# The long projection of a two-sequence encoder layer laid out beside both attentions, with other buffer counts

## The chip, the cores and the metric

The kernel runs on one core of one Trainium2 chip. Its engines are TensorE (PE, with the loads of its stationary operand shown as PEld), VectorE (DVE), ScalarE (ACT), GpSimd (POOL) and SyncE (SP), which issues the DMAs of this kernel. The metric is the device time of one execution in microseconds (us), the median of several runs.

## The reference

One layer of a bidirectional encoder is applied to two sequences with shared weights: a long one of 1024 tokens (s = 0) and a short one of 512 (s = 1), each with 16 learned meta tokens in front. The width is 1024, everything is float32.

```python
def mixer_sublayer(x, ...):
    n = rms_norm(x, g_mix)
    proj = n @ w_in                        # columns: qa, ka, va, qb, kb, vb
    # group A: 8 query heads over 2 key heads, rms-normed q and k, 2-D rotary
    s = jnp.einsum('bqhgd,bkhd->bhgqk', qblk, ka) * scale
    oa = jnp.einsum('bhgqk,bkhd->bqhgd', jax.nn.softmax(s, axis=-1), va)
    # group B: 4 differential heads, two softmax maps each, 1-D rotary
    a = p[:, :, 0] - lam * p[:, :, 1]
    ob = rms_norm(jnp.einsum('bhqk,bkhe->bqhe', a, vb), g_subln) * (1.0 - lam_init)
    return x + jnp.concatenate([oa, ob], axis=-1) @ w_out

def conv_glu_sublayer(x, ...):
    n = rms_norm(x, g_ffn)
    gate = depthwise_conv3(n @ w_ff_gate) + conv_b
    return x + (jax.nn.gelu(gate) * (n @ w_ff_up)) @ w_ff_down

# both sublayers, then rms_norm(h, g_final); the meta tokens are dropped
```

## The kernel before

Each float32 operand of the dense products is split in two halves of float32r (hi and lo), and three matmuls (`mm3`, L111 to L113) make one product: hi by hi, lo by hi, hi by lo. The work is written as Python generators, one for each stage of each sequence:

- `projection(s)` loads x, normalizes it, and makes 18 blocks of 128 columns of the combined projection: first ten for group A's q and k and for the values (each block of q or k with a per-head norm), then eight for group B's keys and queries. The long sequence has three chunks a block, 384, 384 and 272 columns wide. Results go to DRAM as `qk` and `v`.
- `attention(s)` loads keys (`k`, from pool `ak`), queries (`q`) and values (`v`) from DRAM. `softmax` makes one tile of rows `p` (pool `ap`): scores `ps_s` in PSUM (L386, L387), scaled into `p` with its maximum (L388), exponential on ACT (L393), and in group A a scaling by the inverse sum (L462). `weighted_v` transposes four such tiles (three or two in group B) key chunk by key chunk (`ps_t`, L411), splits them, and multiplies them by the values into `ps_o` (L425, L426; L421 to L423 in group B; L435 for the tail of the keys). `ps_o` has one buffer. Long attention has 16 blocks of four tiles in group A and 12 of three pairs in group B.
- `mixer_out` and `conv_glu` are the short sequence's out projection and feed-forward with its final norm. In the final norm (`finish`, L769 and on) sixteen tiles `y` are made from `h` and stored to `yT` (L785).
- `mixer_out_long` and `conv_glu_long` are the long sequence's. The first goes over three parts of the tokens. After each part `combine` makes that part's row norm and the inputs of a seven-product scheme for 2 by 2 blocks, which it keeps in tiles `x11` to `t4`. Those tiles exist from `begin()` on, which drains the short generator and releases its memory.

The order of a stage that has two generators is written with `merge`: it takes the next piece of whichever generator is less far in units that the generators yield, divided by the two weights given.

```python
    i = 0 if b is None or done[0] / wa <= done[1] / wb else 1
```

This is the order of the program text. The planner of the language then orders the instructions of each engine by an estimated timeline in which an instruction that is ready can pass an earlier one that is not; earlier text has priority. Tiles come from pools with a number of buffers, laid out from the left or the right end of on-chip memory, and an instruction that needs a buffer waits until the tile that had that memory is released. All DMAs go through one queue in order (SP).

The top level (`trunk_kernel`, L1138 and on) runs the short projection, then short attention merged with the long projection (weights `R1`) and the rest of that projection by itself, then long attention merged with the short out projection and feed-forward (`R2`), then the long out projection merged with what is left of the short stages (`R3`), then the long feed-forward. PSUM has two accumulators `mm`, three `s`, two `t` and one `o` until the long feed-forward.

Of the kernel before, what the change touches and what calls it, by code (L numbers as in the profile page):

```python
# [12 lines left out]
F32 = mybir.dt.float32  # L13
# [7 lines left out]
P = 128  # L21
# [64 lines left out]
def pool(ctx, g, name, bufs, side):  # L86
    return ctx.enter_context(g.tc.tile_pool(name=name, bufs=bufs, side=side, reuse_waits="tile"))
# [252 lines left out]
def attention(ctx, g, s, side):  # L340
# [4 lines left out]
    nch = len(kch)  # L345
    nf = n // P
    sp = pool(ctx, g, f"as{s}", 8, side)
    kp = pool(ctx, g, f"ak{s}", 4, side)
    qp = pool(ctx, g, f"aq{s}", 3, side)
    vp = pool(ctx, g, f"av{s}", 2, side)  # L350
    pp = pool(ctx, g, f"ap{s}", 9, side)
    ptp = pool(ctx, g, f"apt{s}", 3 if s == 0 else 2, side)
    op = pool(ctx, g, f"ao{s}", 2, side)
    def stacked(tl, j, m, first, c0, cw):
# [12 lines left out]
    def load_k(j, m):  # L367
        k = kp.tile([P, n], F32R, name="k", tag="k")
        stacked(k, j, m, 0, 0, n)
        return k  # L370
# [76 lines left out]
    for kv in range(2):  # L447
        k = load_k(KA, kv)
# [63 lines left out]
    for h in range(4):  # L512
# [3 lines left out]
        for blk in blocks:  # L516
# [3 lines left out]
            ob = yield from diff_block(qs, ks, v, [(c - c0, m) for c, m in blk])  # L520
# [17 lines left out]
def mean_rsqrt(g, tp, out, acc, cw, tag="mm"):  # L538
    ps = g.psum.tile(P, cw, tag)
    g.nc.tensor.matmul(ps, lhsT=g.ones_d, rhs=acc, start=True, stop=True)  # L540
    rsqrt_newton(g, tp, out, ps, cw)
# [148 lines left out]
def conv_glu(ctx, g, s, st, side, wp, wb, gb):  # L690
# [18 lines left out]
    ap = pool(ctx, g, f"fa{s}", 2, side)  # L709
    centres = even_chunks(N, 510)  # L710
    for f0 in range(0, NFF, G):
# [52 lines left out]
        op = pool(ctx, g, f"fo{s}", 2, side)  # L764
        ob = 2 - s
        cw = 256
        yv = g.yT[s].rearrange("(k p) t -> p k t", p=P)

        def finish(c0, acc, sums):  # L769
            rs = rstd[:, 1 + c0:1 + c0 + cw]  # L770
            if sums:
                rsqrt_newton(g, op, rs, acc, cw)
            else:
                mean_rsqrt(g, op, rs, acc, cw)
            for k in range(KT):
                y = op.tile([P, ob, cw], F32, name="y", tag="y", bufs=2 if s == 1 else 4) if k % ob == 0 else y
                hs, gk = h[:, k, 1 + c0:1 + c0 + cw], g.gain[:, V_GFIN + k:V_GFIN + k + 1]
                if k % 4 == 3:
                    nc.scalar.activation(y[:, k % ob], hs, AF.Copy, scale=gk)
                    nc.gpsimd.tensor_tensor(out=y[:, k % ob], in0=y[:, k % ob], in1=rs, op=ALU.mult)  # L780
                else:
                    nc.vector.scalar_tensor_tensor(out=y[:, k % ob], in0=hs, scalar=gk, in1=rs,
                                                   op0=ALU.mult, op1=ALU.mult)
                if (k + 1) % ob == 0:
                    nc.sync.dma_start(out=yv[:, k + 1 - ob:k + 1, c0:c0 + cw], in_=y)  # L785

        waiting = None
        for c0 in range(0, N, cw):
# [3 lines left out]
            for j in range(KT):  # L792
# [5 lines left out]
                else:  # L798
                    add_square(g, op, acc, h, j, 1 + c0, cw, nc.gpsimd if j < PADD else nc.vector, ob)
                if j == LAG and waiting:  # L800
                    finish(*waiting)
# [302 lines left out]
def merge(a, wa, b, wb):  # L1104

    done = [0.0, 0.0]
    while True:
        i = 0 if b is None or done[0] / wa <= done[1] / wb else 1
        try:
            done[i] += next((a, b)[i])  # L1110
        except StopIteration:
            if i == 0:
                break
            b = None


def drain(gen):
    for _ in gen:
        pass


LAG = 5
PADD = 8
ML = 2
K2 = 8
# [5 lines left out]
AF_ = 4  # L1131
LAGF = 5
TS = ("x11", "x21", "t2", "t1", "t3", "x22", "t4")
R1, R2, R3 = (1.0, 0.9), (1.0, 0.4), (1.0, 20.0)


@with_exitstack
def trunk_kernel(ctx, tc, g):  # L1138
    nc = tc.nc
    g.nc, g.tc = nc, tc  # L1140
    const = ctx.enter_context(tc.tile_pool(name="const", bufs=1))
    dram = ctx.enter_context(tc.tile_pool(name="dram", bufs=1, space=DRAM))
    g.qk, g.v, g.vt, g.oT = [], [], [], []
    for s, N in enumerate(SEQS):
        n = N + NMETA
        g.qk.append([dram.tile([3, P, n], F32, name=f"qk{s}_{i}") for i in range(13)])
        g.v.append([dram.tile([P, n // P, 2 * P], F32, name=f"v{s}_{i}") for i in range(5)])

        g.vt.append(dram.tile([5, 96, 2 * P], F32, name=f"vt{s}"))
        g.oT.append(dram.tile([D, N + 1], F32, name=f"oT{s}"))  # L1150

    g.h = dram.tile([KT, P, SEQS[0]], F32, name="h0")

    g.wo = {j: dram.tile([2, P, D], F32, name=f"wo{j}") for j in PRE}
    g.act = dram.tile([NFF // 2, len(TS), P, H], F32, name="act0")
    nc.scalar.preload_act_table_set(EXP_LN)
    g.vec = const.tile([P, V_N], F32, name="vec")
    nc.sync.dma_start(out=g.vec, in_=g.vec_in)
    g.ident = const.tile([P, P], F32, name="ident")
    make_identity(nc, g.ident)  # L1160
    g.ones_d = const.tile([P, P], F32, name="ones_d")
    nc.vector.memset(g.ones_d, 1.0 / D)
    g.ones_v = const.tile([P, P], F32, name="ones_v")
    nc.vector.memset(g.ones_v, 1.0 / P)
    g.ones_hd = const.tile([P, P], F32, name="ones_hd")
    nc.vector.memset(g.ones_hd, 0.0)
    for r in range(4):
        for c in (r % 2, r % 2 + 2):
            nc.vector.memset(g.ones_hd[r * 32:(r + 1) * 32, c * 32:(c + 1) * 32], 1.0 / HD)
    g.gsub = const.tile([P, 1], F32, name="gsub")  # L1170
    nc.vector.tensor_scalar(out=g.gsub, in0=g.vec[:, V_GSUB:V_GSUB + 1], scalar1=-0.5 * (1.0 - LAM_INIT),
                            scalar2=None, op0=ALU.mult)

    g.eps = const.tile([P, 1], F32, name="eps")
    nc.vector.memset(g.eps, EPS)

    g.eps_d = const.tile([P, P], F32, name="eps_d")
    nc.vector.tensor_scalar(out=g.eps_d, in0=g.ident, scalar1=EPS * D * D, scalar2=None, op0=ALU.mult)

    g.gain = const.tile([P, V_CW], F32, name="gain")  # L1180
    nc.vector.tensor_scalar(out=g.gain, in0=g.vec[:, :V_CW], scalar1=-0.5, scalar2=None, op0=ALU.mult)

    prod = const.tile([P, 2, HD], F32, name="prod")
    dots = const.tile([P, 2], F32, name="dots")
    lv = g.vec[:, V_LAM:].rearrange("p (m x c) -> p m x c", m=2, x=2)
    nc.vector.tensor_tensor(out=prod, in0=lv[:, :, 0, :], in1=lv[:, :, 1, :], op=ALU.mult)
    nc.vector.tensor_reduce(out=dots, in_=prod, axis=AX.X, op=ALU.add)
    nc.scalar.activation(dots, dots, AF.Exp)
    g.neglam = const.tile([P, 1], F32, name="neglam")
    nc.vector.tensor_tensor(out=g.neglam, in0=dots[:, 1:2], in1=dots[:, 0:1], op=ALU.subtract)  # L1190
    nc.vector.tensor_scalar(out=g.neglam, in0=g.neglam, scalar1=LAM_INIT, scalar2=None, op0=ALU.subtract)

    def state(es, s, side, with_x):
        C = SEQS[s] + 2
        st = Ctx()
        hp = pool(es, g, f"fh{s}", 1, side)
        if with_x:
            st.x = [hp.tile([P, KT, C], F32R, name=nm) for nm in ("xhi", "xlo")]
        st.h = hp.tile([P, KT, C], F32, name="h")
        st.rstd = hp.tile([P, C], F32, name="rstd")  # L1200
        return st

    g.psum = Psum(tc, "psa", mm=2, s=3, t=2, o=1)
    with ExitStack() as es:
        drain(projection(es, g, 1, "right", "s", "t"))
    with ExitStack() as es0:
        p0 = projection(es0, g, 0, "left", "mm", "mm")
        with ExitStack() as es1:
            merge(attention(es1, g, 1, "right"), R1[0], p0, R1[1])
        drain(p0)  # L1210
    es1, es_x, es_h, x = ExitStack(), ExitStack(), ExitStack(), {}
    wp = pool(es1, g, "fw1", 2, "left")
    st1 = state(es1, 1, "left", True)

    def sample():
        yield from mixer_out(g, 1, st1, "left", wp, 3, "mm")
        yield from conv_glu(es1, g, 1, st1, "left", wp, 3, 1)
    f1 = sample()
    with ExitStack() as es0:
        merge(attention(es0, g, 0, "right"), R2[0], f1, R2[1])  # L1220
    wp0 = pool(ctx, g, "fw0", 2, "right")

    def begin():
        drain(f1)
        es1.close()
        return pool(es_x, g, "fx0", 1, "left")

    late = []

    def long():  # L1230
        late.append((yield from mixer_out_long(es_h, g, wp0, x, begin)))

    merge(long(), R3[0], f1, R3[1])
    g.psum.es.close()
    g.psum = Psum(tc, "psb", mm=8)
    drain(conv_glu_long(ctx, g, wp0, x, late[0], es_x, es_h))
    g.psum.es.close()
# [61 lines left out]
```

## Time and profile before

| What | us |
| --- | --- |
| median of 3 runs | 2171.62 |
| lowest and highest run | 2170.51, 2171.93 |
| the profiled execution, its time | 2172.56 |
| the profiled execution, its span | 2170.8 |
| PE busy in the span | 2061.3 |
| DVE busy in the span | 1732.8 |
| ACT busy in the span | 1164.9 |

The span runs from the first to the last instruction. The granted clock of TensorE is 0.973 of full speed as a mean over the span. Stages named below go by times from the span's start. In a table by stage each row has the stretch, its length, the busy time of each engine with the count of its instructions, the granted clock, the share of time that the DMA engines were busy, and what they moved. In a list of waits a row has the waiting engine, tile and line, what it waited for, the total, the times and the longest. In an order of time a row has the start, the duration, the engine, the line, the operation, the tiles, the shape and the count, and in brackets the idle time before it with what ended it.

### The profile page before, as it was taken

The numbers are of one execution on the slowest core, as the hardware profiler recorded it, in microseconds if no ns is written. First come the engines' busy times: TensorE is split into PE (matmuls) and PEld (weight loads), VectorE is DVE, ScalarE is ACT, GpSimd is POOL, SyncE is SP. The second block draws the span as 40 slices with busy tenths as digits, with TensorE's granted clock in tenths as the row PEclk, the third lists the DMA queues.
The fourth block names the chain that finished last, engine by engine and source line by source line (L and its number), as shares of the span: only waits on it lengthen the run. The fifth ranks groups of instructions, "written<-read, shape, count | busy, mean of one in ns | idle before, by whom it ended". The sixth has DMA issues, their size and how long they took to land.

```text
span 2170.8 us, 35171 instructions
## 1 busy us (share of the span) xinstructions
PE 2061.3 (95%) x12298; PEld 1842.5 (85%) x12298; DVE 1732.8 (80%) x3794; ACT 1164.9 (54%) x2265; POOL 564.1 (26%) x490
## 2 busy tenths in 40 slices
PE   6999999998999999999999999878999999989997
PEld 6898888997887999899999999867887777778877
DVE  6877888866979788889998874569878878869786
ACT  6534665544667556667666654345444444435454
POOL 3464222453112000000000002323444444420112
PEclk9999999999999999999999999977999999999999
DMA  6455334457521322233333236961222232257343
GB/s 231 157 180 179 117 112 145 158 176 243 194 85 54 103 74 70 67 91 111 104 103 99 75 136 175 280 199 41 106 103 83 100 109 83 99 183 244 121 124 124
DMA packets 165954, 284.24 MB, mean 131 GB/s; under 512 B 20848, under 2 KB 90000, under 8 KB 165264
## 3 DMA queue, kind: packets, MB, share of 16 engines
q1 hardware_dynamic: 165776, 281.99, 40.1%
q8 instruction: 97, 1.59, 0.3%
q14 instruction: 81, 0.66, 0.1%
HBM read 202.75 MB, written 79.18 MB: 130 GB/s over the span
## 4 chain that ended last, share of the span: by engine, by line
PE 71%; DVE 15%; DMA 4%; issue 4%; ACT 4%; POOL 1%; SPq 1%; DVEq 0%; POOLq 0%; ACTq 0%
PE ps_mm L111 16%; PE ps_mm L113 16%; PE ps_mm L112 16%; PE ps_t L411 5%; PE ps_s L386 3%; PE ps_s L387 3%; DVE w_lo L106 2%; PE ps_o L426 2%; PE ps_s L111 1%; PE ps_o L425 1%; PE ps_s L113 1%; PE ps_s L112 1%; DVE acc L872 1%; DVE p L388 1%; DMA yT<-y 1%
## 5 line engine op out<-in xcount | busy, mean ns | idle before, releaser
L111 PE MATMUL ps_mm<-xhi,w_hi 128*128 128x258 f32 (+3 forms) x1264 | 389.5, 308 | 12.9 <-ACT xhi L216 7.3
L112 PE MATMUL ps_mm<-xlo,w_hi 128*128 128x258 f32 (+3 forms) x1264 | 381.4, 302 | 4.3 <-DVE xlo L217 3.5
L113 PE MATMUL ps_mm<-xhi,w_lo 128*128 128x258 f32 (+3 forms) x1264 | 379.8, 301 | 0.0
L388 DVE TENSOR_SCALAR_CACHE_REDUCE p<-ps_s 114x344 f32<-114x344 f32 (+4 forms) x562 | 256.7, 488 | 36.1 <-PE ps_s L387 18.3
L393 ACT ACTIVATE p<-p,nm 114x1040 f32<-114x1040 f32 (+5 forms) x212 | 215.0, 1014 | 82.3 <-DVE nm L391 81.3
L111 PEld LDWEIGHTS ps_mm<-xhi,w_hi 128*128 128x128 f32 x1264 | 241.4, 191 | 19.9 <-ACT xhi L216 8.2
L106 DVE TENSOR_TENSOR w_lo<-w_f,w_hi 128x1024 fp32r<-128x1024 f32 (+1 forms) x180 | 192.6, 1077 | 80.1 <-ACT w_hi L105 78.8
L105 ACT CAST pt_hi<-ps_t 128x512 fp32r<-128x512 f32 (+6 forms) x360 | 170.0, 483 | 154.8 <-PE ps_t L411 134.5
L112 PEld LDWEIGHTS ps_mm<-xlo,w_hi 128*128 128x128 f32 x1264 | 241.5, 191 | 8.5 <-DVE xlo L217 4.2
L113 PEld LDWEIGHTS ps_mm<-xhi,w_lo 128*128 128x128 f32 x1264 | 241.2, 191 | 0.8
L105 ACT CAST w_hi<-w_f 128x1024 fp32r<-128x1024 f32 (+1 forms) x197 | 165.1, 856 | 85.6 <-PE ps_mm L112 50.0
L106 DVE TENSOR_TENSOR pt_lo<-ps_t,pt_hi 128x512 fp32r<-128x512 f32 (+4 forms) x312 | 171.6, 560 | 30.2 <-ACT pt_hi L105 28.7
L386 PE MATMUL ps_s<-k,q 128*114 128x348 f32 (+4 forms) x552 | 180.9, 333 | 10.1 <-DVE p L388 9.7
L106 POOL TENSOR_TENSOR a_lo<-gate,a_hi 128x256 fp32r<-128x256 f32 x44 | 42.7, 970 | 549.3 <-ACT a_hi L105 528.6
L411 PE MATMUL ps_t<-ident,p 128*128 128x128 f32 (+7 forms) x1188 | 181.9, 268 | 1.1 <-DVE p L462 0.7
L387 PE MATMUL ps_s<-k,q 128*114 128x348 f32 (+4 forms) x552 | 170.8, 314 | 0.0
L411 PEld LDWEIGHTS ps_t<-ident,p 128*128 128x128 f32 (+7 forms) x1188 | 139.7, 135 | 28.1 <-issue 6.4
L111 PE MATMUL ps_s<-xhi,w_hi 128*128 128x256 f32 (+4 forms) x480 | 150.3, 316 | 13.6 <-ACT xhi L216 7.3
L112 PE MATMUL ps_s<-xlo,w_hi 128*128 128x256 f32 (+4 forms) x480 | 149.9, 313 | 2.3 <-DVE xlo L106 2.2
L113 PE MATMUL ps_mm<-t_hi,w_lo 128*128 128x512 f32 (+2 forms) x368 | 145.4, 395 | 5.2 <-DVE w_lo L106 5.1
L105 ACT CAST w_hi<-w_s 128x512 fp32r<-128x512 f32 x114 | 69.7, 618 | 149.0 <-POOL w_s L817 108.9
L113 PE MATMUL ps_s<-xhi,w_lo 128*128 128x256 f32 (+4 forms) x480 | 148.3, 310 | 0.6 <-DMA w_lo<-wo 0.6
(256 smaller groups left out, 5395.5 us busy)
## 6 DMA issues: line engine op xcount, KB each, us to landing
w_f<-w_gate SPq DMA_DIRECT2D x44, 512.0 KB, 3.3
w_f<-w_up SPq DMA_DIRECT2D x44, 512.0 KB, 3.4
w_f<-w_in SPq DMA_DIRECT2D x36, 512.0 KB, 3.9
a_f<-act SPq DMA_DIRECT2D x64, 256.0 KB, 2.7
w_f<-w_down SPq DMA_DIRECT2D x22, 512.0 KB, 3.4
act<-a_t SPq DMA_DIRECT2D x44, 256.0 KB, 2.1
a<-w_down SPq DMA_DIRECT2D x42, 256.0 KB, 5.3
w_hi<-wo SPq DMA_DIRECT2D x36, 256.0 KB, 4.6
```

Source lines behind the costliest of these rows:

```text
L105: nc.scalar.copy(hi, src)
L106: (lo_engine or nc.vector).tensor_tensor(out=lo, in0=src, in1=hi.bitcast(F32), op=ALU.subtract)
L111: nc.tensor.matmul(ps, lhsT=whi, rhs=xhi, start=start, stop=False)
L112: nc.tensor.matmul(ps, lhsT=whi, rhs=xlo, start=False, stop=False)
L113: nc.tensor.matmul(ps, lhsT=wlo, rhs=xhi, start=False, stop=stop)
L386: nc.tensor.matmul(ps, lhsT=q[0], rhs=k[:, c0:c0 + cw], start=True, stop=False)
L387: nc.tensor.matmul(ps, lhsT=q[1], rhs=k[:, c0:c0 + cw], start=False, stop=True)
L388: nc.vector.tensor_scalar(out=p[:, c0:c0 + cw], in0=ps, scalar1=HD ** -0.5, scalar2=-3.0e38, op0=ALU.mult, op1=ALU.max, accum_out=mx[:, i: ...
L393: nc.scalar.activation(p, p, AF.Exp, bias=nm, accum_out=l)
L411: nc.tensor.transpose(tps[:, c:c + M], p[:, k0:k0 + kw], g.ident[:M, :M])
L425: nc.tensor.matmul(o, lhsT=v[:, i, :], rhs=hi, start=i == 0, stop=False)
L426: nc.tensor.matmul(o, lhsT=v[:, i, :], rhs=lo, start=False, stop=False)
```

## The change

The short stages' generator now begins with the long projection, whose pools it opens and closes itself, and the pools of the short out projection are opened when that is done. This one generator is merged with short attention and then with long attention, so what is left of the long projection is not drained between the two but laid out beside long attention, ahead of the short out projection. The weights are 1.25 in place of 0.9 for the first merge and 0.45 in place of 0.4 for the second. Long attention has three key buffers in place of four and seven row tiles `p` in place of nine; short attention keeps four and nine. The short final norm has twelve buffers `y` in place of two.

```diff
@@ attention
-    kp = pool(ctx, g, f"ak{s}", 4, side)
+    kp = pool(ctx, g, f"ak{s}", 4 if s == 1 else 3, side)
...
-    pp = pool(ctx, g, f"ap{s}", 9, side)
+    pp = pool(ctx, g, f"ap{s}", 9 if s == 1 else 7, side)
@@ conv_glu, finish
-                y = op.tile([P, ob, cw], F32, name="y", tag="y", bufs=2 if s == 1 else 4) if k % ob == 0 else y
+                y = op.tile([P, ob, cw], F32, name="y", tag="y", bufs=YB if s == 1 else 4) if k % ob == 0 else y
@@
+YB = 12
...
-R1, R2, R3 = (1.0, 0.9), (1.0, 0.4), (1.0, 20.0)
+R1, R2, R3 = (1.0, 1.25), (1.0, 0.45), (1.0, 20.0)
@@ trunk_kernel
-    with ExitStack() as es0:
-        p0 = projection(es0, g, 0, "left", "mm", "mm")
-        with ExitStack() as es1:
-            merge(attention(es1, g, 1, "right"), R1[0], p0, R1[1])
-        drain(p0)
     es1, es_x, es_h, x = ExitStack(), ExitStack(), ExitStack(), {}
-    wp = pool(es1, g, "fw1", 2, "left")
-    st1 = state(es1, 1, "left", True)
-
-    def sample():
+
+    def beside():
+
+        with ExitStack() as es:
+            yield from projection(es, g, 0, "left", "mm", "mm")
+        wp = pool(es1, g, "fw1", 2, "left")
+        st1 = state(es1, 1, "left", True)
         yield from mixer_out(g, 1, st1, "left", wp, 3, "mm")
         yield from conv_glu(es1, g, 1, st1, "left", wp, 3, 1)
-    f1 = sample()
-    with ExitStack() as es0:
-        merge(attention(es0, g, 0, "right"), R2[0], f1, R2[1])
+    f1 = beside()
+    for s, ratio in ((1, R1), (0, R2)):
+        with ExitStack() as es0:
+            merge(attention(es0, g, s, "right"), ratio[0], f1, ratio[1])
```

## The prediction

> **What bounds the kernel now.** I read the page's first and fourth parts, then a table of busy time by stage, then the waits and the order of time at the places where that table shows TensorE (PE) idle. The page first: the busy shares and the chain that ended last.
>
> ```profile
> span 2170.8 us, 35171 instructions
> PE 2061.3 (95%) x12298; PEld 1842.5 (85%) x12298; DVE 1732.8 (80%) x3794; ACT 1164.9 (54%) x2265; POOL 564.1 (26%) x490
> PE 71%; DVE 15%; DMA 4%; issue 4%; ACT 4%; POOL 1%; SPq 1%; DVEq 0%; POOLq 0%; ACTq 0%
> ```
>
> PE carries the end: 95% busy, and 71% of the chain. No matmul is added or removed by the change, so it can only fill PE's idle time, or make more of it. Where that idle time lies is in the table by stage (length of the stretch, then each engine's busy time, granted clock, DMA share, GB/s).
>
> ```profile
> core 0: us, PE busy (x) PEld busy (x) DVE busy (x) ACT busy (x) POOL busy (x), PEclk, DMA share, GB/s
> 185.00:400.00 215.00, 199.55 (x1232) 179.83 (x1231) 184.00 (x598) 127.99 (x308) 63.38 (x62) 0.95 0.44 138
> 400.00:520.00 120.00, 119.54 (x810) 118.47 (x810) 79.18 (x195) 51.48 (x126) 59.59 (x55) 1.00 0.50 165
> 520.00:560.00 40.00, 32.18 (x171) 25.15 (x169) 37.62 (x130) 25.98 (x50) 4.08 (x7) 0.91 0.81 274
> 720.00:1280.00 560.00, 559.84 (x3867) 522.54 (x3866) 482.99 (x1332) 361.61 (x650) 34.40 (x40) 1.00 0.28 88
> 1360.00:1400.00 40.00, 39.59 (x262) 38.85 (x261) 24.82 (x49) 16.39 (x39) 13.14 (x17) 1.00 0.91 270
> 1400.00:1440.00 40.00, 26.13 (x116) 23.68 (x115) 21.15 (x37) 14.85 (x28) 5.67 (x7) 0.74 0.79 247
> 1440.00:1520.00 80.00, 64.12 (x326) 58.69 (x325) 71.97 (x92) 43.49 (x88) 30.62 (x20) 0.81 0.27 83
> ```
>
> Short attention with the long projection beside it (185 to 400) leaves 15.4 us idle. The rest of that projection (400 to 520) and almost all of the long attention (720 to 1280) are full. Two places are left that the change touches: the hand-over at 520 to 560, with 7.8 us idle and a clock of 0.91, and 1400 to 1440, with 13.9 us idle and a clock of 0.74.
>
> **The long projection and the ratios.** The source says that short attention is laid out with 0.9 units of the long projection to each of its own, and the rest is drained after it. Counting the yields, short attention is 211.7 thousand units and the projection 459.7, so at 0.9 the program text has 41% of the projection beside attention, and at 1.25 it has 58%. The profile does not follow the text. Matmuls into the projection's accumulators, by stretch:
>
> ```profile
> 0.00:185.00 185.00, 33.69 (x155) 26.81 (x156) 7.20 (x13) 4.21 (x8) 0.94 0.57 189
> 185.00:348.00 163.00, 93.50 (x482) 79.77 (x481) 19.66 (x39) 9.65 (x21) 0.96 0.40 127
> 348.00:510.00 162.00, 122.42 (x686) 108.93 (x686) 40.14 (x79) 3.85 (x9) 0.98 0.49 159
> 510.00:521.00 11.00, 9.27 (x59) 8.75 (x57) 3.60 (x7) 0.00 (x0) 1.00 0.93 280
> ```
>
> Of 1382 matmuls, 1323 (96%) are done by 510, when attention's last value product runs (below). The planner lets the projection run ahead wherever PE is free, and it is ahead of both ratios all the way. So attention has the earlier place in the text under 0.9 and under 1.25 alike, and I price the new first ratio at nothing. Its ends are a gain of the 15.4 us idle at 185 to 400, and a loss of the same size if the order gets worse. The second ratio gets nothing for the same reason: the short layers' feed-forward is nearly through when long attention ends (24.6 us of it are left, row below), though 0.4 would have laid out 320 of its 910 thousand units. The "drain" hardly exists in time, so its removal gains no 42% of a projection.
>
> **The hand-over.** What the layout can move is the start of long attention. Its first steps, on SyncE's queue (SP) and on PE:
>
> ```profile
> 446.13 0.53 SPq L357 DMA_DIRECT2D k<-qk  x1
> 510.69 0.53 SPq L357 DMA_DIRECT2D q<-qk  x1
> ```
> ```profile
> 509.21 0.31 PE L435 MATMUL ps_o<-pt_hi,v_tail 96*128 96x306 f32 x1
> 519.92 0.29 PE L113 MATMUL ps_mm<-xhi,w_lo 128*128 128x272 f32 x1
> 520.05 0.32 PE L386 MATMUL ps_s<-k,q 128*128 128x348 f32 x1
> ```
>
> Its keys come at 446, its queries only at 510.69, after short attention's last value product at 509.21, and its first scores follow the projection's last matmul within 0.2 us. Meanwhile DVE had 40.8 of 120 us free (400 to 520), and then it is busy 37.62 of 40. In the changed text long attention's buffers must fit beside the projection's, which is what the smaller pools buy, so queries and first softmaxes no longer wait for the projection's memory. They still wait for short attention's. The hand-over costs 7.8 us idle and 0.09 x 40 = 3.6 us of clock, 11.4 together. What does not go away:
>
> ```profile
> PE ps_mm L111 <- ACT xhi L105: 4.6, 4, 2.0
> ```
>
> 4.6 us are the out projection waiting for its own split inputs, loaded into the projection's old memory. I take 11.4 - 4.6 = 6.8 us gained; ends 0 and 11.4. The moved instructions are the same in number: DMAs of keys, queries and values, which now stand in SP's queue among the projection's stores. A query load that waits for its buffer there would hold the stores behind it, and the projection's u and hi tiles with them; the planner places loads when their buffers are free, so I price that at nothing, and without that the loss is the hand-over's 11.4 us again. GpSimd (POOL), which makes the projection's lo halves and would copy attention's halo, was busy 59.6 of 120 us there and has room.
>
> **Fewer row tiles and keys.** Long attention has 7 row tiles (p) in place of 9, and 3 keys in place of 4. A row tile is already waited for:
>
> ```profile
> 834.23 0.32 PE L386 MATMUL ps_s<-k,q 128*128 128x348 f32 x1
> 845.79 0.60 PE L411 MATMUL ps_t<-ident,p 128*32 128x128 f32 x4
> 846.10 0.52 DVE L388 TENSOR_SCALAR_CACHE_REDUCE p<-ps_s 128x348 f32<-128x348 f32 x1
> ```
>
> Scores made at 834.23 are read at 846.10, right after the block's last transposes free its four tiles. With 7, a block of four can have three of the next block's tiles ready, and the fourth is made after that point. One softmax, from the groups by shape:
>
> ```profile
> L388 DVE TENSOR_SCALAR_CACHE_REDUCE p<-ps_s 128x348 f32<-128x348 f32 x128 | 62.9, 511 | 12.9 <-PE ps_s L387 6.6 <-PE ps_t L411 5.7
> L393 ACT ACTIVATE p<-p,nm 128x1040 f32<-128x1040 f32 x64 | 74.6, 1166 | 25.0 <-DVE nm L391 24.6 <-DVE res L574 0.3
> L462 DVE TENSOR_SCALAR p<-p,r 128x1040 f32<-128x1040 f32 x64 | 48.4, 757 | 0.6
> ```
>
> 3 x 0.511 + 1.166 + 0.757 = 3.5 us, for 16 blocks 55 us by which attention could be later. PE stays covered as long as the feed-forward beside it lasts. Of that, this is left when long attention ends (its matmuls from 1316 on):
>
> ```profile
> 1316.00:1384.00 68.00, 24.56 (x177) 22.78 (x176) 9.56 (x23) 0.46 (x1) 1.00 0.81 232
> ```
>
> So the ends are 0, and 55 - 24.6 = 30 us lost. I take 0, because PE is busy 559.84 of 560 us in that stage and DVE 483, so the delay has cover. A fourth key load would wait behind a key in use and hold SP's queue, query and weight loads with it; four head changes, covered by the same work. No gain is in it: fewer buffers start nothing earlier.
>
> **Twelve output tiles.** The short final norm writes sixteen tiles through two. Waits on DVE, its order of time, and PE's waits there:
>
> ```profile
> DVE y L782 <- DMA yT<-y: 12.0, 5, 3.3
> ```
> ```profile
> 1403.44 0.48 DVE L782 SCALAR_TENSOR_TENSOR y<-h,gain,rstd 128x256 f32<-128x256 f32 x1 [3.01 <-DMA yT<-y]
> 1403.85 0.51 DVE L675 TENSOR_TENSOR h<-ps_s,res 128x344 f32<-128x344 f32 x1
> 1424.30 1.65 DVE L106 TENSOR_TENSOR x_lo<-h,x_hi 128x680 fp32r<-128x680 f32 x2 [1.15 <-ACT x_hi L105]
> ```
> ```profile
> PE ps_s L605 <- DVE h L675: 8.1, 1, 8.1
> PE ps_s L605 <- POOL acc L535: 6.1, 1, 6.1
> PE ps_mm L113 <- DVE w_lo L106: 5.6, 3, 4.5
> ```
>
> DVE stands 12.0 us behind stores of y, and the long out projection's h (1403.85) stands behind it; the stores themselves are issued later, with the next weight loads behind them in SP's queue. The split of the long gate's inputs starts at 1424.30, when the last y has read the short h, and PE's 8.1 us wait follows it. With twelve tiles no y waits. The most that can come back is 13.9 us idle and 0.26 x 40 = 10.4 us of clock, 24.3. The other two waits lie after 1440 and stay. What is late next is the DMA: at 0.79 the stretch has 31.6 us of transfers, which at the 0.91 of the stretch before take 34.7, so if loads are all that is left 5.3 us come back. Between 5.3 and DVE's 12.0 I take the mean, 8.7; ends 0 and 24.3.
>
> The Trainium skill (Perfetto Trace Analysis, Roofline) gives about 435 GB/s as the ceiling of one core's 16 DMA engines. By that the stretch's 247 GB/s would be no limit, the 12.0 us would come back whole, and the sum would be 3.3 us lower. The row has the engines 0.91 busy at 270 GB/s, so I stay with the row.
>
> **Sum.** The profiled execution took 2172.6 us, 0.9 above the median of 2171.6. 2172.6 - 6.8 + 0 - 8.7 = 2157.1, and against the median 2156.
>
> **Rivals.** *Slower: row tiles.* If the full 3.5 us a block lies on attention's path, it ends 55 us later, the feed-forward beside it runs out, and 30 us are lost: 2156 + 30 = 2186. It turns to slower once the delay passes 24.6 + 15.5 = 40 us, 2.5 a block. For it speaks the wait at 846.10. Against it, the next block's value products need the one output accumulator (o), evacuated after the last transposes too, which hides part of the 3.5. The Trainium skill (Trainium Kernel Development and Optimization, Best Practices) says that consistent bubbles can mean that SBUF ran out; by that this rival would be likelier, and the trace agrees at 846.10, but PE shows no bubble from 720 to 1280.
> *Nothing: it does not do what it says.* The projection ends beside attention already, short attention's own memory holds long attention's queries as before, and DMA covers the y stalls: 2171.
> *Larger.* Hand-over and y stretch come back whole: 2171.6 - 11.4 - 24.3 = 2136.
>
> **Chances.** Forecast 0.50 (its own range 2145 to 2166), larger 0.16, nothing 0.16, slower 0.18. Range 2133 to 2181: half of the larger and half of the slower case lie outside. A change of under 0.2% (4.3 us) cannot be told from none. Faster 0.50 + 0.16 + 0.06 of the third case = 0.72, same 0.10, slower 0.18.
>
> **What would show it.** Right: queries of long attention and its first scores before the projection's last matmul; PE busier than 32.2 in the 40 us after that matmul; no wait of y for a store, and the wait of 8.1 us gone or short. The p delay shows in the distance of one block's last value product to the next. Wrong: attention's end later than the feed-forward's, with PE idle before it; or DMA above 0.9 and PE no busier after the last y.

## Result and the profile after

| | before | after |
| --- | --- | --- |
| median of 4 runs, us | 2171.74 | 2206.97 |
| lowest and highest, us | 2170.51, 2171.93 | 2202.56, 2209.20 |
| ratio, 95% interval | | 1.0161 (1.0143 to 1.0179) |
| profiled span, us | 2170.8 | 2200.8 |

The change made the kernel 1.6% slower, 35 us, where 15.5 us of gain were forecast. A profile is of one execution, which can lie some us from the median: 2202.56 us here, 2165.62 with twelve tiles y (below), 2175.31 with the new layout and nine row tiles (below). The first page of the kernel after:

```profile
span 2200.8 us, 35177 instructions
PE 2068.0 (94%) x12298; PEld 1842.5 (84%) x12298; DVE 1740.3 (79%) x3794; ACT 1164.3 (53%) x2265; POOL 568.1 (26%) x490
PE 67%; DVE 14%; DMA 7%; issue 4%; ACT 4%; POOL 2%; SPq 1%; DVEq 0%; POOLq 0%; ACTq 0%
```

The work is the same; PE's share of the chain fell from 71% to 67% and that of DMA rose from 4% to 7%. The table by stage of the kernel after says where (columns as before):

```profile
520.00:560.00 40.00, 32.56 (x175) 25.84 (x175) 33.77 (x111) 26.58 (x50) 1.26 (x3) 0.87 0.77 262
720.00:1280.00 560.00, 559.14 (x3859) 518.99 (x3858) 470.42 (x1266) 349.77 (x616) 39.01 (x42) 1.00 0.29 90
1280.00:1320.00 40.00, 36.58 (x268) 35.42 (x267) 36.95 (x108) 25.85 (x62) 13.66 (x17) 0.95 0.17 54
1320.00:1360.00 40.00, 28.90 (x157) 23.54 (x157) 29.09 (x85) 24.65 (x56) 3.05 (x4) 0.88 0.11 37
1360.00:1400.00 40.00, 24.26 (x127) 22.41 (x126) 9.56 (x31) 8.35 (x17) 2.75 (x3) 0.76 0.81 238
1400.00:1440.00 40.00, 34.26 (x192) 31.98 (x191) 15.28 (x29) 11.91 (x23) 5.65 (x6) 0.93 0.97 304
1440.00:1520.00 80.00, 66.53 (x362) 63.65 (x361) 65.51 (x91) 39.76 (x79) 28.25 (x18) 0.88 0.63 192
```

PE is as full from 720 to 1280 as before (559.14 against 559.84), and nothing in that row warns of the loss. It breaks at 1280 to 1400, where PE is 89.7 of 120 us busy and was 118.2 before (the third row, 39.59, stands in the prediction). Before:

```profile
1280.00:1320.00 40.00, 39.69 (x276) 36.66 (x275) 24.27 (x46) 18.98 (x34) 1.07 (x1) 1.00 0.49 163
1320.00:1360.00 40.00, 38.92 (x272) 38.65 (x272) 16.98 (x44) 15.58 (x34) 12.82 (x15) 1.00 0.80 227
```

The short feed-forward's last product ends at 1313.3 (1383.3 before), attention's last value product comes at 1358.2 (1315.7 before), and PE has idle time between: the sign of being wrong that the prediction named. DVE's count in 720 to 1280 does warn: 1266 instructions in place of 1332. Attention got on more slowly under a full PE. That is seen in the last value products of its blocks, here two neighbouring blocks of group A, the end of group A (the small product of 8 columns), and the end of attention. Before:

```profile
823.75 0.50 PE L435 MATMUL ps_o<-pt_hi,v_tail 64*128 64x512 f32 x1
850.75 0.50 PE L435 MATMUL ps_o<-pt_hi,v_tail 64*128 64x512 f32 x1
978.38 0.27 PE L435 MATMUL ps_o<-pt_hi,v_tail 64*128 64x8 f32 x1
1315.69 0.32 PE L435 MATMUL ps_o<-pt_hi,v_tail 96*128 96x342 f32 x1
```

And after:

```profile
830.39 0.50 PE L435 MATMUL ps_o<-pt_hi,v_tail 64*128 64x512 f32 x1
859.21 0.49 PE L435 MATMUL ps_o<-pt_hi,v_tail 64*128 64x512 f32 x1
1029.41 0.27 PE L435 MATMUL ps_o<-pt_hi,v_tail 64*128 64x8 f32 x1
1358.19 0.42 PE L435 MATMUL ps_o<-pt_hi,v_tail 96*128 96x342 f32 x1 [0.58 <-ACT pt_hi L433]
```

From its first block's last value product (559.8 before, 555.8 after) to its end group A took 418.6 us and takes 473.6: 55.0 more, 3.4 a block as a mean (the two blocks shown are 1.8 us further apart). Group B took 337.3 and takes 328.8. With the start 4.0 us earlier, attention ends 42.5 us later. The order of time inside one block after, on PE and DVE, shows why:

```profile
813.20 0.32 PE L386 MATMUL ps_s<-k,q 128*128 128x344 f32 x1
823.17 0.60 PE L411 MATMUL ps_t<-ident,p 128*32 128x128 f32 x4
824.41 0.52 DVE L388 TENSOR_SCALAR_CACHE_REDUCE p<-ps_s 128x348 f32<-128x348 f32 x1
827.31 0.32 PE L386 MATMUL ps_s<-k,q 128*128 128x348 f32 x1
```

Three tiles of the next block are ready. The last scores of its fourth are made at 813.20, and no tile `p` is left for them; the last transposes of the running block begin at 823.17, and 1.2 us later, at 824.41, those scores go to a row tile. No further score product runs until 827.31.

### The profile page after: what moved, and what is told of

Its sections match the earlier page's. It is cut to its first block, busy times and chain, and to the rows that moved or that the text cites. A ratio compares the mean times of both kernels' runs of the same rounds, so it can differ in the third digit from the quotient of the medians.

```text
span 2200.8 us, 35177 instructions
## 1 busy us (share of the span) xinstructions
PE 2068.0 (94%) x12298; PEld 1842.5 (84%) x12298; DVE 1740.3 (79%) x3794; ACT 1164.3 (53%) x2265; POOL 568.1 (26%) x490
## 4 chain that ended last, share of the span: by engine, by line
PE 67%; DVE 14%; DMA 7%; issue 4%; ACT 4%; POOL 2%; SPq 1%; DVEq 0%; POOLq 0%; ACTq 0%
PE ps_mm L112 15%; PE ps_mm L113 15%; PE ps_mm L111 15%; PE ps_t L411 5%; PE ps_s L386 3%; PE ps_s L387 3%; DVE w_lo L106 2%; PE ps_o L426 2%; DMA w_f<-w_in 2%; PE ps_o L425 1%; DVE p L388 1%; DMA m<-oT 1%; DVE acc L872 1%; DMA w_hi<-wo 1%; PE ps_s L111 1%
## 5 line engine op out<-in xcount | busy, mean ns | idle before, releaser
L106 DVE TENSOR_TENSOR w_lo<-w_f,w_hi 128x1024 fp32r<-128x1024 f32 (+1 forms) x180 | 197.5, 1104 | 76.8 <-ACT w_hi L105 71.1
L411 PE MATMUL ps_t<-ident,p 128*128 128x128 f32 (+7 forms) x1188 | 187.3, 270 | 1.2 <-DVE p L462 0.8
L111 PE MATMUL ps_s<-xhi,w_hi 128*128 128x256 f32 (+4 forms) x480 | 150.4, 319 | 32.8 <-ACT xhi L105 15.5
```

The costliest lines, as they stand in the source:

```text
L106: (lo_engine or nc.vector).tensor_tensor(out=lo, in0=src, in1=hi.bitcast(F32), op=ALU.subtract)
L111: nc.tensor.matmul(ps, lhsT=whi, rhs=xhi, start=start, stop=False)
L411: nc.tensor.transpose(tps[:, c:c + M], p[:, k0:k0 + kw], g.ident[:M, :M])
```

## Experiments

All ratios are to the kernel before, run on the same chip, with 95% intervals.

**One part at a time.** First seven row tiles:

```diff
-    pp = pool(ctx, g, f"ap{s}", 9, side)
+    pp = pool(ctx, g, f"ap{s}", 9 if s == 1 else 7, side)
```

> The kernel before with seven row tiles p for long attention and nothing else. Theory (row tiles): each of the 16 blocks of group A ends one softmax, about 3.4 us, later; attention ends 40 to 55 us later, the short feed-forward beside it runs out and PE is idle after it. Time 2195 to 2210 us. Rival (the layout of the projection beside both attentions, or the ratios): no change here, 2172 us within 4. Rival (keys): no change here either.

Measured 2189.95 us, 1.0093 (1.007 to 1.0115): slower, by 20 us, a little below what was expected. The blocks are those of the whole change:

```profile
1030.67 0.27 PE L435 MATMUL ps_o<-pt_hi,v_tail 64*128 64x8 f32 x1
1357.01 0.42 PE L435 MATMUL ps_o<-pt_hi,v_tail 96*128 96x342 f32 x1 [0.57 <-ACT pt_hi L433]
```

So the two tiles make nearly all of attention's delay, 41.3 of 42.5 us at its end, but not the whole 35 us. Three keys:

```diff
-    kp = pool(ctx, g, f"ak{s}", 4, side)
+    kp = pool(ctx, g, f"ak{s}", 4 if s == 1 else 3, side)
```

> The kernel before with three key buffers for long attention and nothing else. Theory (row tiles): within 0.2% of 2172 us, attention's end moves by less than 5 us. Rival (keys): a key load that waits for a buffer holds SP's queue at the head changes, and group A or B gets longer; 2185 to 2205 us.

Measured 2172.43 us, 1.0015 (1.0001 to 1.0029): 3 us by the ratio, hardly more than none, and attention's end moved by 1.1 us. Twelve tiles y:

```diff
-                y = op.tile(..., bufs=2 if s == 1 else 4) if k % ob == 0 else y
+                y = op.tile(..., bufs=12 if s == 1 else 4) if k % ob == 0 else y
```

> The kernel before with twelve buffers y in the short final norm and nothing else. By the prediction's step: the 12.0 us in which DVE waits for stores of y go, PE's wait of 8.1 us goes or gets short, 2163 us (2148 to 2172). Rival (DMA covers it): 2172 us. Theory of the loss (row tiles): this part is not slower.

Measured 2158.08 us, 0.9947 (0.9931 to 0.9964): 11.5 us faster. No y of the short norm waits for a store any more, PE's wait of 8.1 us for h is gone, and the two stretches are, in a profiled execution 6.9 us shorter than the one before:

```profile
1360.00:1400.00 40.00, 35.92 (x221) 33.98 (x220) 25.01 (x47) 16.41 (x39) 13.81 (x17) 0.96 0.87 264
1400.00:1440.00 40.00, 33.91 (x193) 31.74 (x192) 29.19 (x49) 17.98 (x33) 8.11 (x8) 0.91 0.88 272
```

1400 to 1440 has 33.9 us of PE in place of 26.1 and a clock of 0.91 in place of 0.74; 1360 to 1400 has 3.7 us less. The new weights:

```diff
-R1, R2, R3 = (1.0, 0.9), (1.0, 0.4), (1.0, 20.0)
+R1, R2, R3 = (1.0, 1.25), (1.0, 0.45), (1.0, 20.0)
```

> The kernel before with the new weights, 1.25 and 0.45, and nothing else: the rest of the projection is still drained between the attentions. Theory (row tiles) and the prediction's step: within 0.2% of 2172 us, since the projection runs ahead of both weights. Rival (layout and ratios): the order gets worse where the two attentions meet, 2180 us or more.

Measured 2169.25 us, 0.9994 (0.998 to 1.0008): no change. The four parts add to about +10 us, so some 25 of the 35 were still without a cause.

**What comes after attention.** With seven tiles alone the long out projection's first weights and its first inputs `m` are issued at these times (SP's queue):

```profile
1342.57 0.38 SPq L156 DMA_DIRECT2D w_hi<-wo  x1
1357.28 0.38 SPq L659 DMA_DIRECT2D m<-oT  x1
```

In the kernel after:

```profile
1358.64 0.32 SPq L156 DMA_DIRECT2D w_hi<-wo  x1
1366.81 0.38 SPq L659 DMA_DIRECT2D m<-oT  x1
```

The first weight comes 0.45 us after attention's last value product (1358.19), where with seven tiles it came 14.4 us ahead of it (1357.01), and the inputs queue behind. A memory theory follows from the tile sizes in the source (KB of 1024 bytes a partition; no run shows the addresses themselves): these weights (ten tiles of 2 KB and two of 4 KB, 28 KB) are opened from the same end of memory as attention. With four keys (16.3 KB) and the queries (12.0 KB) they reach no further than these; with three keys they reach up to 4 KB into the values too, which attention reads to its end. The waits of SP's queue agree: the first of these loads waits 5.9 us for the last value product (L435) in the kernel after, and with seven tiles alone none waits for that product.

```diff
+    kp = pool(ctx, g, f"ak{s}", 4 if s == 1 else 3, side)
+    pp = pool(ctx, g, f"ap{s}", 9 if s == 1 else 7, side)
```

> The kernel before with seven row tiles and three keys. Theory (row tiles, and a shift of memory): with seven tiles alone the long out projection's first weight load came at 1342.6, with the whole change at 1358.6, because without the fourth key everything behind the keys lies one tile (4 KB) lower and those weights reach into memory that attention uses to its end. That costs nothing while the short feed-forward still covers it, as with three keys alone, and 10 to 13 us once it does not. So 2200 to 2207 us, first weight load at about 1358. Rival (the parts add up): 2190 + 2 = 2192 us. Rival (layout of the projection): 2192 us, the rest of the loss in the layout.

Measured 2205.01 us, 1.0166 (1.0143 to 1.0189): the parts do not add up. The same with an unused tile in the place of the fourth key:

```diff
+    if s == 0:
+        gap = pool(ctx, g, "gap", 1, side).tile([P, n], F32, name="gap")
+        nc.vector.memset(gap[:, 0:1], 0.0)
```

> Seven row tiles, three keys, and an unused tile of the size of a key behind the keys, so that all later memory lies where it did before. Theory (shift of memory): first weight load of the long out projection at about 1343 again, 2188 to 2193 us. Rival (the missing key buffer itself holds a load): as with seven tiles and three keys without the gap, whatever that gives.

Measured 2187.82 us, 1.0087 (1.0074 to 1.0101). Their first weights, three keys and then three keys with the gap:

```profile
1356.95 0.33 SPq L156 DMA_DIRECT2D w_hi<-wo  x1
```

```profile
1339.77 0.38 SPq L156 DMA_DIRECT2D w_hi<-wo  x1
```

17 us come from where the later tiles lie; 10 to 13 were expected. None can be seen from the missing buffer as a buffer: with the gap the ratio is 1.0087, with seven tiles alone 1.0093. With three keys the first load again waits for the last value product, 7.2 us; with the gap none does. The stretch 1360 to 1400 shows the same, three keys first, then with the gap:

```profile
1360.00:1400.00 40.00, 24.75 (x122) 23.24 (x121) 9.59 (x31) 8.37 (x17) 2.74 (x3) 0.73 0.81 239
```

```profile
1360.00:1400.00 40.00, 34.68 (x195) 32.72 (x193) 13.19 (x34) 9.72 (x21) 5.52 (x6) 0.91 0.83 227
```

With three keys and nine tiles the first weights were late too (1317.2 in place of 1275.8) and it cost 3 us: the short feed-forward still covered it. In the kernel after the late loads stand in PE's waits from 1280 to 1560 in place of the 8.1 us:

```profile
PE ps_s L111 <- ACT xhi L105: 15.5, 3, 12.2
PE ps_s L111 <- DMA w_hi<-wo: 7.4, 5, 2.3
```

All three buffer counts with the old layout and weights:

```diff
+    kp = pool(ctx, g, f"ak{s}", 4 if s == 1 else 3, side)
+    pp = pool(ctx, g, f"ap{s}", 9 if s == 1 else 7, side)
+                y = op.tile(..., bufs=12 if s == 1 else 4) if k % ob == 0 else y
```

> The kernel before with all three buffer counts of the change (7 row tiles, 3 keys, 12 y), but the old layout and weights: the projection drained between the attentions. Theory: attention ends after the short norm, so y's stores are hidden and the twelve buffers bring nothing; 2198 to 2207 us, as with the whole change. Rival (the parts add up, the layout is to blame for the rest): 2190 + 2 - 12 = 2180 us.

Measured 2201.98 us, 1.0152 (1.0138 to 1.0166): the loss of the whole change. The twelve y bring next to nothing here (1.0166 without them, intervals overlapping): in the kernel after the short norm runs from 1312.7 to 1333.8, while attention still has until 1358.2, and nobody waits for it.

**How much one row tile costs.** Eight and six, each alone:

```diff
+    pp = pool(ctx, g, f"ap{s}", 9 if s == 1 else 8, side)     # 6 in the run after it
```

> The kernel before with eight row tiles for long attention. Theory (a block of four waits for its fourth tile only if fewer than eight are there): all four tiles of the next block can be made ahead, blocks keep the distance of before within 1 us, attention ends within 12 us of before, 2172 us within 6. Rival (loss in proportion to the buffers): half of that of seven, 2181 us.

Measured 2172.21 us, 1.0007 (0.9998 to 1.0016): no change. Its group A takes 418.5 us, as with nine (418.6). Its attention ends 10.5 us later, at 1326.15, under the short feed-forward; half of that is there when short attention ends (514.6 against 509.2), the rest arises in group B.

> The kernel before with six row tiles for long attention. Theory (a block of four has only as many tiles of the next block ready as there are beyond four, and each one missing puts a softmax of 3.5 us on the way): two are missing, group A gets 110 us longer than before in place of 55; group B gives back what it did with seven, about 11 us; attention ends at about 1412, and less the 24.6 us of short feed-forward that covered the first part, 72 us are lost: 2235 to 2250 us, more if group B, with three pairs of tiles a block, also runs short. Rival (loss in proportion to the buffers, 8 us each from nine on): 2195 us. Rival (PE, full until 1280, absorbs it): below 2190 us.

Measured 2239.37 us, 1.0314 (1.0286 to 1.0341): as expected. Ends of group A and of attention:

```profile
1089.87 0.27 PE L435 MATMUL ps_o<-pt_hi,v_tail 64*128 64x8 f32 x1
1398.27 0.42 PE L435 MATMUL ps_o<-pt_hi,v_tail 96*128 96x342 f32 x1 [0.79 <-ACT pt_hi L433]
```

From its first block (555.9) group A takes 534.0 us, 115 more than before (110 expected). Group B, with PE to itself after the short norm's last y, which ends at 1294.2, takes 308.4 in place of 337.3, so attention ends 14 us sooner than expected. Nine, eight, seven, six tiles: 0, 1.5, 20, 68 us. For group A the cost begins below twice its block of four.

**The layout alone.** Nine tiles fit into the new layout with one buffer of values:

```diff
-    vp = pool(ctx, g, f"av{s}", 2, side)
+    vp = pool(ctx, g, f"av{s}", 2 if s == 1 else 1, side)
-    pp = pool(ctx, g, f"ap{s}", 9 if s == 1 else 7, side)
+    pp = pool(ctx, g, f"ap{s}", 9, side)
```

> The changed kernel with nine row tiles again, and one buffer of values in place of two so that it fits; three keys, twelve y and the new layout and weights stay. Theory (the loss is the row tiles and what they uncover): attention ends before 1325 again, the twelve y gain their 12 us, 2158 to 2165 us. Rival (the layout itself costs): 2170 us or more. To be read beside the next one, which has the same buffers and the old layout.

Measured 2170.64 us, 0.9997 (0.9984 to 1.0011). The same buffers in the old layout:

```diff
 # the kernel before, with
+    vp = pool(ctx, g, f"av{s}", 2 if s == 1 else 1, side)
+    kp = pool(ctx, g, f"ak{s}", 4 if s == 1 else 3, side)
+                y = op.tile(..., bufs=12 if s == 1 else 4) if k % ob == 0 else y
```

> The kernel before with one buffer of values, three keys and twelve y: the buffers of the run above, old layout and weights. Theory: as the run above within 0.2%, 2158 to 2165 us, since the long projection runs ahead of the text in both. By the prediction's step for the hand-over the new layout would be 6.8 us faster than this. Rival (the layout costs): this is faster by 5 us or more.

Measured 2163.63 us, 0.9967 (0.995 to 0.9983). So the new layout with its weights costs 7 us (the intervals just miss each other) where the theory said none. The last run moved more of the projection ahead:

```diff
 # the new layout with nine tiles, and
-R1, R2, R3 = (1.0, 1.25), (1.0, 0.45), (1.0, 20.0)
+R1, R2, R3 = (1.0, 2.0), (1.0, 0.45), (1.0, 20.0)
```

> The new layout with nine row tiles (one buffer of values, three keys, twelve y) and a first weight of 2.0 in place of 1.25, so that 92% of the long projection, not 58%, stands in the text beside short attention and little of it beside long attention. Theory (the layout costs 7 us because long attention's first products and the projection's last blocks compete where they are laid out together): 2164 us, as with the old layout. Rival (the cost is in something else of the layout, as where the pools of the short out projection open): 2171 us again.

Measured 2197.77 us, 1.012 (1.0101 to 1.0139): neither. Table by stage around the hand-over, in this order: old layout, new layout, new layout with 2.0:

```profile
505.00:545.00 40.00, 33.79 (x185) 27.22 (x183) 30.81 (x101) 20.22 (x41) 9.90 (x14) 0.98 0.83 282
545.00:585.00 40.00, 39.82 (x281) 36.53 (x282) 33.73 (x98) 23.88 (x46) 3.77 (x6) 0.98 0.58 195
```

```profile
505.00:545.00 40.00, 35.24 (x201) 32.61 (x201) 26.62 (x84) 16.08 (x33) 12.02 (x16) 0.87 0.73 247
545.00:585.00 40.00, 36.38 (x246) 31.75 (x245) 35.31 (x111) 26.92 (x51) 2.50 (x5) 1.00 0.62 207
```

```profile
505.00:545.00 40.00, 25.05 (x117) 21.51 (x115) 19.72 (x57) 17.15 (x39) 4.58 (x8) 0.66 0.75 254
545.00:585.00 40.00, 37.72 (x256) 33.26 (x256) 36.23 (x122) 26.21 (x51) 3.38 (x6) 1.00 0.47 143
```

With 2.0 the projection ends at 507.4, 15.7 us before short attention's last value product (523.1), and nothing is left to cover the hand-over: 25 of 40 us busy. So the projection's tail beside the hand-over is of use, and pulling it forward is the wrong cure. Why the new layout at 1.25 loses 7 us is not settled. Part of it is in these rows (71.6 us of PE in 505 to 585 against 73.6, and a clock of 0.87 in the first). In these two profiled executions, 11.7 us apart, short attention's last value product also comes 5.4 us later in the new layout (514.5 against 509.1), and group A takes 7.0 us more (420.1 against 413.1). Short attention's end alone lies anywhere from 505.3 to 514.6 in the runs with the old layout and weights, so one profile of each does not tell the layout from chance.

**A version that beats both kernels** is the kernel before with twelve y alone, 2158.08 us.

## Why the prediction was wrong, step by step

*Ratios.* Priced at nothing; 0.9994 measured. Right for these two weights. The reason, that the projection runs ahead and attention keeps the earlier place, does not carry to every weight: at 2.0 the projection passed attention, and the time was 2197.77 us.

*The hand-over.* 6.8 us of gain were taken; this step failed. What it named came true: queries at 504.5 and first scores at 511.07, 4.7 us before the projection's last matmul at 515.82. But nothing was gained by it: in the 40 us after the projection's last matmul PE is busy 30.5 us, where the prediction asked for more than 32.2, at a clock of 0.87 against 0.91. From short attention's last value product to that of the first long block it takes 51.6 us (504.15 to 555.8), 50.6 before. The earlier scores were put among the projection's products, and the queries still follow short attention's end. With like buffers the layout costs 7 us, inside the bound of 11.4 given for a loss; why, stays open.

*Fewer row tiles and keys.* Priced at nothing, and this is the step that decided. The time of one softmax a block, 3.5 us and 55 in all, was sized right: 55.0 measured in group A, and 115 for two tiles fewer. The error was in choosing zero because PE is full from 720 to 1280. That PE is full says that the short work fills what attention leaves; it does not say how much short work there is. The row that answers was in the prediction: 24.6 us of it were left at attention's end. With seven tiles alone 41.3 us of delay less 24.6 are 17, and 20 were measured; with eight 10.5 us stay below 24.6, and nothing was lost; with six 82.6 less 24.6 are 58, and 68 were measured. So this difference gives the bulk of the loss, and some us more come on top. The slower rival had the mechanism; it lacked that group B would give 8.5 us back, and the memory behind the keys (next). The Trainium skill (Trainium Kernel Development and Optimization, Best Practices) says that consistent bubbles can mean that SBUF, the on-chip memory, ran out. Here row tiles ran out and PE showed no bubble, 559.14 of 560 us busy; the sign was that the blocks of group A lay 3.4 us further apart as a mean.

*The keys.* The prediction looked at the buffer as a buffer (a fourth load that waits) and priced it at nothing. It missed that a pool made smaller moves every tile behind it, and what is opened there later: 17 us by the run with the gap.

*Twelve y.* 8.7 us forecast, 11.5 (7.8 to 15.0) measured alone: mechanism right, and the size inside the interval, which also holds the 12.0 of DVE's waits. The lower bound of 5.3, by which loads were all that is left, was too low; DMA's share in that stretch is 0.88 with twelve y. By the 435 GB/s that the Trainium skill (Perfetto Trace Analysis, Roofline) gives, the 12.0 would come back whole; 11.5 is nearer to that, but the interval does not decide. The ceiling itself is not seen here: DMA is 0.97 busy at 304 GB/s in the row 1400 to 1440 after. In the whole change the gain was nothing, since the short norm no longer stood at the end.

*The sum.* -6.8 + 0 - 8.7 became: 19 for the row tiles (seven tiles with the gap), 17 for the memory behind the keys, between -3 and 0 for the y, and about 2 for the layout and weights (1.0152 without them, 1.0161 with them, which the intervals cannot tell from none), against a measured 35.

## What to carry to other kernels

A full engine hides a delay only as long as the other stream has work: compare the delay with what that stream has left where the delayed one ends, not with how full the engine is on the way. In the blocks of four shown here, buffers cost nothing until fewer than two blocks' worth were left, and then each missing buffer cost about one step in every block. Making a pool smaller also moves every later tile, so look at what the next stage's first loads will lie on, and try an unused tile in the gap to tell the two apart.

## What the runs showed of the hardware

The granted clock falls where PE idles: 0.73 to 0.76 with PE 24 to 25 of 40 us busy (1360 to 1400 in the kernel after and with seven tiles and three keys), 0.66 in 505 to 545 with the weight 2.0. These are means over stretches that hold the idle time too. The matmuls behind the idle time are slower as well: in the kernel after, behind PE's wait of 12.2 us, the clock is 0.62 from 1370 to 1380 and a product of 342 columns takes 0.49 us (at 1374.89), against 0.32 us at a clock of 1.00 (at 1351.97, stretch 1351 to 1354). So a stretch that waits for loads has fewer busy us of PE, and some of those are at a lower clock.
